# Low parts of y, of the output weights and of the late weights computed on VectorE instead of POOL, and the seventh pair's y split where it is gated

## The chip, the cores and the metric

The kernel runs on one core of a Trainium2 chip. Its time is the device time of one execution in microseconds (us), taken as the median of several runs; lower is better. In the profile TensorE appears as PE (its weight loads as PEld), VectorE as DVE, ScalarE as ACT, GpSimd as POOL, and SyncE, which here only starts DMAs, as SP. Each engine works through its own list of instructions in order, so an instruction that waits holds up everything behind it on that engine.

## The reference

Two residual layers over a sequence of 1024 positions and a width of 1024, all in float32: a gated linear recurrence (RG-LRU, width 1536), then a forgetting attention with 16 heads of 64, each followed by an output projection, and a final RMS norm. Cut to what matters here:

```python
# layer 0
h = rms_norm(x, norm_g[0]);  u = h @ lru_w_in
xb, gate = u[..., :1536], u[..., 1536:]
xc = causal_depthwise_conv(xb, conv_w, conv_b)
r, i = sigmoid(block_diag(xc, wa, ba)), sigmoid(block_diag(xc, wx, bx))
a = exp(-8 * r * softplus(-a_param))
hs = scan(a, sqrt(1 - a*a) * (i * xc))        # h_t = a_t h_{t-1} + b_t
x = x + (hs * silu(gate)) @ lru_w_out
# layer 1
h = rms_norm(x, norm_g[1]);  q, k, v, gate, f = split(h @ fox_w_in)
p = softmax(q k^T / 8 + cum_q - cum_k, causal) # 16 heads
x = x + ((p @ v) * silu(gate)) @ fox_w_out
out = rms_norm(x, final_g)
```

## The kernel before

**Split operands.** Every large product is made of three matmuls. An operand z in float32 is split into a high part, `to_hi` (a cast to the type `F32R`), and a low part, `to_lo` (L85/L86: `lo = z - hi`). `gemm_steps` (L101 to L114) then issues, for each block of 128 weights, high times high (L111), low weights times high (L112) and high weights times low (L113), all into one accumulator. So each weight block of 128 by 512 elements needs one cast on ACT (L75) and one subtraction, and each activation needs the same. The helper `weights` (L95) reads a block from DRAM into a tile `wf`, casts it on ACT into `wh` and by default subtracts on POOL into `wl`.

**Layer 0** runs over 12 blocks n of 128 channels (the loop at L364). For each n: the input product `ups`, the gates of the block before (`gates`, PSUM tile `gate`), the y of the block before that (`outputs`, L325), the convolution (`conv`: `us`, `xc`, the split `xch`/`xcl`), the gate-path product `gps`, `silu`, and the recurrence (`recur`, with a scan on DVE). `outputs` multiplies the scan's result by the gate and splits it into `yh` and `yl`, tiles of 128 by 1024. After each second block, `project_out(g)` becomes a list of pieces (`fill`) that are worked off between the blocks: for four pairs of output blocks, `out_weights` (L336) loads and splits 128 by 512 output weights, and four accumulations into `ops` are added to `x`. There are six groups g; groups 0 to 4 go through `project_out`, the last is done at L432. `held` is a dictionary of open `gps` tiles; at L411 it is set to `None`, and `out_weights` looks at that to choose the engine of its low part: VectorE once `held` is `None`, POOL before.

**Layer 1** runs over the 16 heads in pairs (a pair is one block of 128 channels). For each head: `maxima` (scores tile `S` on PE, the row maximum on DVE at L664, the exponential with its sum on ACT at L667, and the row of maxima `mrow` at L673), then `weigh` (transposed scores `ST`, the exponential `p` on ACT at L734 or L737, masking on POOL at L742, its split `ph`/`pl` on DVE at L81 and L86, and the product with V into `O`, L762 and L763). Then `scale` (L701) multiplies the gate path by the reciprocal sums on POOL, after those came through DRAM (`recd`, `recb`), and `gated` (L771) multiplies the head pair's output `yo` by that on POOL, at every odd head and for each half c of the sequence. For pairs 0 to 6 the result is stored in DRAM (`y1d`); `load_y` reads it back later into a tile of tag `xp` and `split_y` splits it into `yhh`/`yhl`, cast on ACT and subtraction on DVE. The last pair, heads 14 and 15, is split directly from `yo`. `run` weaves these generators by the strings in `ORDERS`: digits name a generator, each `.` takes a piece of filler (projections for later pairs; from head 13 on `partial`, the output projection over the first six pairs, with tiles `xp`, `wh`, `wl`) and one of a side list. At head 14 the side list is `late` (L892): it loads and splits the output weights of the last two pairs (`woh` on ACT, `wol` on POOL; 4 blocks of 128 by 512), and then loads and splits the seventh pair's y (pair 6) for both halves. `final` uses pairs 6 and 7.

**Order.** The code is written in one order, but a planner that runs at build time (the context is made with `schedule_with_timeline_sim=True`) fixes the order on each engine: it takes, in written order of precedence, what its own simulation finds ready. `tc.issue_after(x)` holds instructions back until behind x on x's engine. On the chip that order is kept whatever the real durations are.

Of the kernel before, what the change touches and what calls it, by code (L numbers as in the profile page):

```python
# [33 lines left out]
def f32(ap):  # L34
    return ap.bitcast(F32)
# [3 lines left out]
def trunk(ctx: ExitStack, tc: tile.TileContext, xt, w0, wg, wo0, pc, gn, w1, wv, wf, bf, wo1, out):  # L39
    nc = tc.nc  # L40
# [31 lines left out]
    def to_hi(hi, src, eng, scale=None):  # L72
        if eng is nc.scalar:
            if scale is None:
                nc.scalar.copy(hi, src)  # L75
            else:
                nc.scalar.activation(hi, src, AF.Copy, scale=scale)
        elif eng is nc.gpsimd:
            nc.gpsimd.tensor_scalar(hi, src, 1.0 if scale is None else scale, 0.0, ALU.mult, ALU.add)
        elif scale is None:  # L80
            eng.tensor_copy(hi, src)  # L81
        else:
            eng.tensor_scalar(hi, src, scale, None, ALU.mult)

    def to_lo(lo, src, hi, eng):  # L85
        return eng.tensor_tensor(lo, src, f32(hi), ALU.subtract)  # L86
# [30 lines left out]
    def drain(gen):  # L117
        for _ in gen:
            pass
# [49 lines left out]
    with ExitStack() as l0:  # L169
# [57 lines left out]
        def split_x(h, layer=0):  # L227
            for k, (hi, lo) in enumerate((raw, hT)[layer][h]):
                g_ = gnt[:, layer, k : k + 1]
                x = xs[h][k]  # L230
                to_hi(hi, x, nc.scalar, scale=g_)
                nc.vector.scalar_tensor_tensor(lo, x, g_, f32(hi), ALU.mult, ALU.subtract)
                yield
# [91 lines left out]
        def outputs(n, parts=(slice(0, SEQ),), gate=itertools.repeat(None)):  # L325
            s = state.pop(n)
            y = tuple(ypool.tile([P, SEQ], F32R, tag=z, name=z) for z in ("yh", "yl"))
            for cs, _ in zip(parts, gate):
                a_ = s["a"][:, cs]
                nc.vector.tensor_tensor(a_, a_, s["sg"][:, cs], ALU.mult)  # L330
                yh, yl = (z[:, cs] for z in y)
                to_hi(yh, a_, nc.scalar)
                to_lo(yl, a_, yh, nc.vector if len(parts) > 1 else nc.gpsimd)
            ys.append(y)

        def out_weights(g, d0):  # L336

            wt = wpool.tile([P, 4, P], F32, tag="wf", name="wf", bufs=3)
            for j in range(2):
                nc.sync.dma_start(wt[:, 2 * j : 2 * j + 2], wo0[d0 + j, :, 2 * g : 2 * g + 2])  # L340
            hi = wpool.tile([P, 4, P], F32R, tag="wh", name="wh")
            lo = wpool.tile([P, 4, P], F32R, tag="wl", name="wl")
            to_hi(hi, wt, nc.scalar)
            to_lo(lo, wt, hi, nc.vector if held is None else nc.gpsimd)
            return [[(hi[:, 2 * j + i], lo[:, 2 * j + i]) for i in range(2)] for j in range(2)]

        def project_out(g):

            for d0 in range(0, KT, 2):
                for db, w in enumerate(out_weights(g, d0), d0):  # L350
                    for h, cs in enumerate(halves):
                        pt = ps.tile([P, HALF], F32, tag="g", name="ops")
                        gemm(pt, zip(w, [tuple(z[:, cs] for z in p) for p in ys[2 * g : 2 * g + 2]]))
                        x = xs[h][db]
                        nc.vector.tensor_tensor(x, x, pt, ALU.add)  # L355
                        yield
# [6 lines left out]
        ys, fill, held = [], iter(()), {}  # L363
        for n in range(NB):  # L364
# [8 lines left out]
            if n == 0:  # L373
                gps = held[0] = two_banks("gps")
                product(gps[:, 0], 0, first[1])
                for _ in zip(split_x(1), square_x(1)):
                    pass
                done = rms_row(sums[0], rs[:, :HALF])[1]
            else:
                gates(n - 1)  # L380
                if n > 1:
                    with tc.issue_after(state[n - 1]["last"].ins):
                        outputs(n - 2)
# [24 lines left out]
        for h in range(2):  # L408
            product(gps[:, h], h, wn)
        outputs(NB - 2)  # L410
        held = None  # L411
        drain(fill)
        recur(NB - 1, halves)
        outputs(NB - 1, halves, silu(state[NB - 1], gps, halves))
# [11 lines left out]
        def mm3(o, w, x, start, stop):  # L426
# [3 lines left out]
            nc.tensor.matmul(o, wh, xl, start=False, stop=stop)  # L430

        wl = [w for d0 in range(0, KT, 2) for w in out_weights(NB // 2 - 1, d0)]  # L432
        for h, cs in enumerate(halves):
            y = [tuple(z[:, cs] for z in p) for p in ys[-2:]]
            hT[h] = [pair() for k in range(KT)]
            parts = split_x(h, 1)
# [29 lines left out]
    with ExitStack() as l1:  # L466
# [76 lines left out]
        def kq_units(pair, hs=(0, 1)):  # L543

            for is_k in (1, 0):
                if hs[0] == 0:
                    kq[pair, is_k] = tuple(
                        kqpool.tile([P, SEQ], F32R, tag=f"qk{p}{is_k}", name=f"qk{p}") for p in "hl"
                    )
                hi, lo = kq[pair, is_k]  # L550
                eng = nc.vector if pair == 0 else nc.scalar

                def use(h, pt):
                    cs = slice(h * HALF, (h + 1) * HALF)
                    if is_k:
                        to_hi(hi[:, cs], pt, eng)
                        to_lo(lo[:, cs], pt, hi[:, cs], nc.vector)
                    else:
                        to_hi(hi[:, cs], pt, eng, scale=0.125)
                        nc.vector.scalar_tensor_tensor(lo[:, cs], pt, 0.125, f32(hi[:, cs]), ALU.mult, ALU.subtract)  # L560

                yield from project(is_k * 8 + pair, use, hs)
# [30 lines left out]
        parts = [at.tile([HEADS, SEQ], F32R, tag=t, name="cp") for t in ("ph", "pl")]  # L593
# [177 lines left out]
        def gated(hd, c, sub=slice(0, HALF)):  # L771

            if hd % 2 == 0:
                return
            pair = hd // 2
            yo = yos[pair, c][:, sub]
            nc.gpsimd.tensor_tensor(
                yo, yo, sgs[pair][:, c * HALF + sub.start : c * HALF + sub.stop], ALU.mult
            )
            if hd == 15:  # L780
                split_y(c, yo, nc.vector, sub)
            else:
                nc.sync.dma_start(y1d[c, pair], yo)
# [19 lines left out]
        def split_y(c, y, eng, sub=slice(0, HALF)):  # L803
            if sub.start == 0:
                y1[c].append(tuple(hpool.tile([P, HALF], F32R, tag=t, name="y" + t) for t in ("hh", "hl")))
            yh, yl = (z[:, sub] for z in y1[c][-1])
            to_hi(yh, y, nc.scalar)
            to_lo(yl, y, yh, eng)

        def load_y(c, pairs):  # L810
            for pair in pairs:
                y = at.tile([P, HALF], F32, tag="xp", name="y", bufs=3)
                nc.sync.dma_start(y, y1d[c, pair])
                split_y(c, y, nc.vector)
# [77 lines left out]
        def late():  # L892

            for half in range(2):
                wh, wl = (kqpool.tile([P, 8, P], F32R, tag=f"qk{p}{half}", name=f"wo{p}") for p in "hl")
                for b in range(2):
                    wt = wpool.tile([P, 4, P], F32, tag="wf", name="wf", bufs=3)
                    for d in range(2):
                        nc.sync.dma_start(wt[:, 2 * d : 2 * d + 2], wo1[half * 4 + b * 2 + d, :, 6:8])
                    sl = slice(4 * b, 4 * b + 4)  # L900

                    with tc.issue_after(seen[0].ins):
                        to_hi(wh[:, sl], wt, nc.scalar)
                    to_lo(wl[:, sl], wt, wh[:, sl], nc.gpsimd)
                    yield
                late_w.extend([(wh[:, 2 * d + k], wl[:, 2 * d + k]) for k in range(2)] for d in range(4))
            for c in range(2):
                load_y(c, [6])
                yield

        drain(kq_units(0, (1,)))
        fill = g_units(0)
        for _ in range(4):
# [5 lines left out]
        for hd in range(HEADS):  # L919
# [14 lines left out]
            if hd == HEADS - 1:  # L934
                break
            scale(hd)
            gated(hd, 0)
            side = late() if hd == 14 else iter(())
            run(second, weigh(hd, 1), maxima(hd + 1, 0), fill=fill, side=side)
            drain(side)  # L940
            gated(hd, 1)
            if hd == 12:

# [8 lines left out]
        quarters = [slice(0, 256), slice(256, HALF)]  # L952
        scale(15, slice(0, HALF))
        gated(15, 0)
        run("0.....0...0.......0...", weigh(15, 1, quarters[0]), fill=fill)
        drain(fill)
# [82 lines left out]
```

## Time and profile before

| | us |
|---|---|
| median of three runs (lowest, highest) | 1171.12 (1170.85, 1172.95) |
| the profiled execution | 1169.07 |
| its span, first to last instruction | 1167.4 |
| busy in that span: PE, PEld, DVE, ACT, POOL | 1135.0, 949.2, 821.0, 596.3, 394.5 |

The span leaves 1.7 us of the profiled execution outside it, and the profiled execution is 2.05 us below the median. The granted clock of PE is 0.992 on average over the span. A busy share is an average: what a place in the kernel is worth is read from the idle time of PE around it, since PE works on the same matmuls in any case.

### The profile page before, as it was taken

To read this page: it belongs to the slowest core of one execution; us is meant where nothing else is said; L and a number is where in the kernel's file an instruction comes from. 1 tells how busy PE (TensorE), PEld (TensorE's weight loads), DVE (VectorE), ACT (ScalarE), POOL (GpSimd) and SP (SyncE) were. 2 spreads that over 40 slices of the span, in tenths; PEclk is the share of its full clock that TensorE was granted. 3 is DMA by queue.
4 is the path that set the end of the run, shared out by engine and by line. 5 is a ranking of instruction groups with operands and counts; after the bars stand their busy time and mean duration, and the time that the engine had idled before them with its cause. 6 is when DMAs were issued, how large, how long until landed. Compare 5 with 4: busy or idle time off the path is not lost.

```text
span 1167.4 us, 15836 instructions
## 1 busy us (share of the span) xinstructions
PE 1135.0 (97%) x5653; PEld 949.2 (81%) x5653; DVE 821.0 (70%) x1278; ACT 596.3 (51%) x1010; POOL 394.5 (34%) x361
## 2 busy tenths in 40 slices
PE   9998999999999999999999999999999999999996
PEld 7786888888888887978888988889888898787795
DVE  7588746766567779566877767777577775676677
ACT  8386445364453667454554545545455454444343
POOL 1233332342323302342333332333333233143445
PEclk9999999999999999999999999999999999999998
DMA  6111120111111124441343423433234331656544
GB/s 209 51 41 40 51 59 28 59 50 41 55 36 55 54 68 153 108 132 46 92 118 81 102 64 92 119 85 89 64 91 110 90 84 60 184 161 171 160 134 145
DMA packets 63278, 105.95 MB, mean 91 GB/s; under 512 B 8856, under 2 KB 27928, under 8 KB 63200
## 3 DMA queue, kind: packets, MB, share of 16 engines
q1 hardware_dynamic: 63200, 104.95, 32.1%
q8 instruction: 44, 0.72, 0.3%
q14 instruction: 34, 0.28, 0.1%
HBM read 63.30 MB, written 16.45 MB: 68 GB/s over the span
## 4 chain that ended last, share of the span: by engine, by line
PE 48%; DVE 6%; ACT 2%; issue 2%; DMA 1%; DVEq 0%; POOL 0%; ACTq 0%; SPq 0%
PE gps L111 6%; PE gps L112 6%; PE gps L113 6%; PE O L763 3%; PE S L660 3%; PE S L659 3%; PE ST L728 3%; PE O L762 3%; PE ST L729 2%; PE vps L524 2%; PE vps L522 2%; PE vps L523 2%; PE ops L112 2%; PE ops L113 2%; PE ops L111 2%
## 5 line engine op out<-in xcount | busy, mean ns | idle before, releaser
L86 POOL TENSOR_TENSOR wl<-wf,wh 128x512 fp32r<-128x512 f32 (+2 forms) x148 | 216.5, 1467 | 418.3 <-ACT wh L75 376.2
L111 PE MATMUL gps<-hh,wh 128*128 128x512 f32 x576 | 226.9, 394 | 0.6 <-DVE qkl L560 0.5
L112 PE MATMUL gps<-hh,wl 128*128 128x512 f32 x576 | 227.4, 395 | 0.0
L113 PE MATMUL gps<-hl,wh 128*128 128x512 f32 x576 | 227.2, 394 | 0.0
L75 ACT CAST wh<-wf 128x512 fp32r<-128x512 f32 (+2 forms) x156 | 94.1, 607 | 134.6 <-PE ops L113 38.8
L667 ACT ACTIVATE S<-S,st 128x128 f32<-128x128 f32 (+7 forms) x128 | 91.4, 714 | 111.5 <-DVE st L664 110.6
L113 PEld LDWEIGHTS gps<-hl,wh 128*128 128x128 f32 x576 | 108.4, 188 | 24.6 <-issue 0.5
L81 DVE CAST ph<-p 128x512 fp32r<-128x512 f32 (+2 forms) x130 | 83.9, 655 | 61.4 <-ACT p L734 32.3
L111 PEld LDWEIGHTS gps<-hh,wh 128*128 128x128 f32 x576 | 108.5, 188 | 22.6 <-DVE qkl L560 0.9
L112 PEld LDWEIGHTS gps<-hh,wl 128*128 128x128 f32 x576 | 108.4, 188 | 21.9 <-POOL wl L86 0.3
L86 DVE TENSOR_TENSOR pl<-p,ph 128x512 fp32r<-128x512 f32 (+2 forms) x130 | 115.1, 901 | 2.2
L742 POOL TENSOR_SCALAR_AFFINE_SELECT p<-p 128x128 f32<-128x128 f32 (+1 forms) x128 | 46.9, 384 | 190.4 <-ACT p L734 92.0
L664 DVE CUSTOM_DVE_ANT_0 S<-S,mask 128x128 f32<-128x128 f32 (+7 forms) x128 | 96.6, 758 | 9.9 <-PE S L660 8.9
L355 DVE TENSOR_TENSOR x<-x,ops 128x512 f32<-128x512 f32 x80 | 54.3, 682 | 48.7 <-PE ops L113 48.4
L111 PE MATMUL ups<-hh,wh 128*128 128x512 f32 x192 | 76.3, 397 | 2.6 <-DVE us L265 1.9
L112 PE MATMUL ups<-hh,wl 128*128 128x512 f32 x192 | 75.6, 394 | 0.8 <-POOL wl L86 0.8
L113 PE MATMUL ups<-hl,wh 128*128 128x512 f32 x192 | 76.0, 396 | 0.2
L734 ACT ACTIVATE p<-ST 128x512 f32<-128x512 f32 (+1 forms) x68 | 53.0, 786 | 42.5 <-PE ST L729 39.1
L524 PE MATMUL vps<-wl,hh 128*128 128x256 f32 (+1 forms) x256 | 72.2, 284 | 0.7 <-POOL wl L86 0.7
L522 PE MATMUL vps<-wh,hh 128*128 128x256 f32 (+1 forms) x256 | 72.5, 285 | 0.0
L523 PE MATMUL vps<-wh,hl 128*128 128x256 f32 (+1 forms) x256 | 72.5, 284 | 0.0
L728 PE MATMUL ST<-U,T 128*128 128x512 f32 (+1 forms) x198 | 67.7, 349 | 2.7 <-ACT S L667 2.7
(193 smaller groups left out, 2611.1 us busy)
## 6 DMA issues: line engine op xcount, KB each, us to landing
wf<-in_w SPq DMA_DIRECT2D x100, 256.0 KB
wf<-in_wo SPq DMA_DIRECT2D x64, 128.0 KB
T<-qkh SPq DMA_DIRECT2D x28, 256.0 KB
U<-qkh SPq DMA_DIRECT2D x28, 256.0 KB
x<-in_xt SPq DMA_DIRECT2D x16, 256.0 KB
x1d<-x SPq DMA_DIRECT2D x16, 256.0 KB
wf<-in_wv SPq DMA_DIRECT2D x16, 256.0 KB
xp<-x1d SPq DMA_DIRECT2D x16, 256.0 KB
```

The source lines that it names most:

```text
L75: nc.scalar.copy(hi, src)
L81: eng.tensor_copy(hi, src)
L86: return eng.tensor_tensor(lo, src, f32(hi), ALU.subtract)
L111: nc.tensor.matmul(o, wh, xh[:, cs], start=i == 0, stop=False)
L112: nc.tensor.matmul(o, wl, xh[:, cs], start=False, stop=False)
L113: nc.tensor.matmul(o, wh, xl[:, cs], start=False, stop=i == len(pairs) - 1)
L522: nc.tensor.matmul(pt, xh, wh, start=k == 0, stop=False)
L523: nc.tensor.matmul(pt, xl, wh, start=False, stop=False)
L524: nc.tensor.matmul(pt, xh, wl, start=False, stop=k == KT - 1)
L664: nc.vector.tensor_tensor_reduce(S[:, :n], S[:, :n], mask[:, SEQ - n :], -1.0, -NEG, ALU.add, ALU.min, accum_out=m)
L667: seen[0] = nc.scalar.activation(S[:, :n], S[:, :n], AF.Exp, bias=f32(m), scale=-1.0, accum_out=sums[:, i : i + 1])
L728: nc.tensor.matmul(A[:, jj, :n], T[s][:, 0, ks], U[s][:, 0, q0:end], start=True, stop=False)
```

## The change

Four edits. `outputs` computes `yl` on VectorE always (before: on POOL, except for the last block, which comes in two halves). `out_weights` computes its low part on VectorE always (before: on POOL until `held` is `None`), and the line `held = None` goes. `late` computes the low part of the late weights on VectorE instead of POOL. And `gated` splits y directly for heads 13 and 15 instead of 15 alone, so pair 6 is no longer stored to `y1d` and read back, and `late` no longer loads it.

```diff
@@ outputs
-                to_lo(yl, a_, yh, nc.vector if len(parts) > 1 else nc.gpsimd)
+                to_lo(yl, a_, yh, nc.vector)
@@ out_weights
-            to_lo(lo, wt, hi, nc.vector if held is None else nc.gpsimd)
+            to_lo(lo, wt, hi, nc.vector)
@@ after the loop of layer 0
         outputs(NB - 2)
-        held = None
         drain(fill)
@@ gated
-            if hd == 15:
+            if hd >= 13:
                 split_y(c, yo, nc.vector, sub)
             else:
                 nc.sync.dma_start(y1d[c, pair], yo)
@@ late
-                    to_lo(wl[:, sl], wt, wh[:, sl], nc.gpsimd)
+                    to_lo(wl[:, sl], wt, wh[:, sl], nc.vector)
                     yield
                 late_w.extend([(wh[:, 2 * d + k], wl[:, 2 * d + k]) for k in range(2)] for d in range(4))
-            for c in range(2):
-                load_y(c, [6])
-                yield
-
```

## The prediction

> **What bounds the kernel now.** I read the busy times first, then a table of stretches, then PE's own waits.
>
> ```profile
> PE 1135.0 (97%) x5653; PEld 949.2 (81%) x5653; DVE 821.0 (70%) x1278; ACT 596.3 (51%) x1010; POOL 394.5 (34%) x361
> ```
>
> ```profile
> 108.00:112.00 4.00, 3.66 (x9) 2.53 (x10) 3.65 (x2) 3.42 (x6) 2.70 (x2) 0.57 0.00 0
> 120.00:150.00 30.00, 30.00 (x132) 24.39 (x130) 20.07 (x22) 9.18 (x12) 11.41 (x6) 1.00 0.13 41
> 1036.00:1056.00 20.00, 20.00 (x97) 16.80 (x96) 13.91 (x21) 7.23 (x15) 10.71 (x12) 1.00 0.63 166
> 1074.00:1084.00 10.00, 7.02 (x30) 4.91 (x31) 9.97 (x7) 4.29 (x8) 9.35 (x7) 1.00 0.40 117
> 1084.00:1089.00 5.00, 5.00 (x18) 3.88 (x19) 4.94 (x12) 2.42 (x5) 2.81 (x4) 0.66 0.80 238
> ```
>
> A row of the second fence is a stretch, its length, then busy us (and instructions) of PE, PEld, DVE, ACT and POOL, PE's granted clock, the DMA share and GB/s. PE is busy 97% of the span, so at most 1167.4 - 1135.0 = 32 us of idle time and a few us of low clock can be won. From 120 us on, PE is full (30.00 of 30) while DVE has 10 us of 30 free: a faster low part there moves nothing. Two places stand out where instructions leave POOL: 96 to 112 us (layer 0, blocks 2 and 3) and 1068 to 1089 us (head 14, where `late` runs). After each the clock falls, to 0.57 over 4 us and 0.66 over 5 us: (1 - 0.57) x 4 = 1.7 us and (1 - 0.66) x 5 = 1.7 us. PE's waits in the two places, by what ended them:
>
> ```profile
> PE gate L111 <- ACT ti L290: 2.2, 1, 2.2
> PE gate L111 <- ACT th L290: 1.9, 1, 1.9
> ```
>
> ```profile
> PE ST L728 <- ACT S L667: 1.8, 1, 1.8
> PE mrow L673 <- DVE st L664: 1.7, 1, 1.7
> PE S L659 <- ACT S L667: 0.6, 1, 0.6
> PE O L762 <- DVE ph L81: 0.6, 1, 0.6
> ```
>
> A row gives us in total, times and the longest. So the early place costs 4.1 us of waiting plus 1.7 of clock, 5.8 together; the late one 4.7 plus 1.7, 6.4 together. These 12 us are what the change can reach.
>
> **The change, part by part.** First the price of the moved subtractions.
>
> ```profile
> L86 POOL TENSOR_TENSOR yl<-a,yh x11: 2392/2406/3121, 85.7 to 410.4; 128x1024 fp32r<-128x1024 f32 x11
> ```
>
> ```profile
> L86 DVE TENSOR_TENSOR wl<-wf,wh x8: 676/681/691, 4.6 to 441.0; 128x512 fp32r<-128x512 f32 x8
> ```
>
> ```profile
> 103.90 0.43 DVE L86 TENSOR_TENSOR wgl<-wgf,wgh 128x256 fp32r<-128x256 f32 x1
> 104.25 1.22 DVE L86 TENSOR_TENSOR xcl<-xc,xch 128x1024 fp32r<-128x1024 f32 x1
> 108.32 1.23 DVE L319 SCALAR_TENSOR_TENSOR ti<-ti,xc 128x1024 f32<-128x1024 f32 x1 [2.86 <-ACT ti L290]
> ```
>
> Eleven `yl` leave POOL (2.41 us each) for DVE, where the same shape (`xcl`) takes 1.22: 13.4 us. Of the 24 blocks of output weights, DVE already does six (its eight `wl` less two at the start of the kernel), so 18 move at 0.68: 12.2 us. Four late blocks: 2.7. DVE gains 28 us of work over 1167.
>
> *Layer 0 after 120 us.* The eleven `yl` lie some 32 us apart (85.7 to 410.4), so one block brings one of them and about two weight blocks, 1.22 + 1.36 = 2.6 us, against 10 us free; PE's full rows cover it, and I cost it at nothing. Without that cover a subtraction on the path would cost its own 0.68 or 1.22.
>
> *The early place.* POOL and DVE get in each other's way:
>
> ```profile
> 85.66 3.12 POOL L86 TENSOR_TENSOR yl<-a,yh 128x1024 fp32r<-128x1024 f32 x1 [5.23 <-ACT yh L75]
> 88.74 1.47 POOL L86 TENSOR_TENSOR wl<-wf,wh 128x512 fp32r<-128x512 f32 x1
> ```
>
> ```profile
> 86.44 2.62 DVE L86 TENSOR_TENSOR wgl<-wgf,wgh 128x256 fp32r<-128x256 f32 x1
> 88.99 2.30 DVE L319 SCALAR_TENSOR_TENSOR ti<-ti,xc 128x1024 f32<-128x1024 f32 x1
> ...
> 95.86 1.19 DVE L265 TENSOR_TENSOR us<-ups,rs 128x1024 f32<-128x1024 f32 x1
> ```
>
> ```profile
> 91.80 0.62 ACT L75 CAST wh<-wf 128x512 fp32r<-128x512 f32 x1 [3.33 <-DMA wf<-in_wo]
> ```
>
> `wgl` took 2.62 instead of 0.43 while POOL wrote `yl`, and `ti` 2.30 instead of 1.23 beside `wl`: 2.19 + 1.07 = 3.26 us lost on an unbroken row of DVE work that ends with `us` at 97.05. ACT's convolution step waits for `us`, and both gate waits of PE (1.9, 2.2) come behind it. With the change these 3.26 go, and one `yl` and two `wl` come (the second behind the cast quoted last), 1.22 + 2 x 0.68 = 2.58: `us` ends 0.68 earlier. Both ends: with both `wl` planned behind `us` the gain is 2.04; with DVE held at the second `wl`, until its cast ends at 92.42, some 1.2 us, `us` comes 0.5 later. I take 0.7 gained, the row nearest to the present order, and leave the second wait and the low clock as they are.
>
> *The late place, the detour of pair 6.* The chain of waits passes through the read of `y1d`:
>
> ```profile
> 1069.98 0.62 ACT L75 CAST yhh<-y 128x512 fp32r<-128x512 f32 x1 [3.02 <-DMA y<-y1d]
> 1070.62 0.56 ACT L667 ACTIVATE S<-S,st 128x384 f32<-128x384 f32 x1
> ```
>
> ACT idles 3.02 us for that read with the exponential L667 queued behind it, and PE's 1.8 us wait is for that exponential. With the split made where y is gated, neither read nor cast is there; the casts go to just behind the two gating products:
>
> ```profile
> 1037.52 2.40 POOL L704 TENSOR_TENSOR sg<-sg,recb 64x1024 f32<-64x1024 f32 x1 [2.54 <-DMA recb<-recd]
> ...
> 1041.56 1.29 POOL L777 TENSOR_TENSOR yo<-yo,sg 128x512 f32<-128x512 f32 x1
> ...
> 1052.84 1.30 POOL L777 TENSOR_TENSOR yo<-yo,sg 128x512 f32<-128x512 f32 x1
> ```
>
> From 1036 to 1056 the table of stretches has ACT busy 7.2 of 20 us, DVE 13.9 and PE full, so 0.62 on ACT and 0.69 on DVE for each half cost nothing; without that cover they would cost 2.6. Two stores, two reads and two tiles of tag `xp` go as well, out of SP's list and out of `partial`'s way. Gain 1.75 (1.8 in the row).
>
> *The late place, the late weights.*
>
> ```profile
> 1074.38 2.85 POOL L704 TENSOR_TENSOR sg<-sg,recb 64x1024 f32<-64x1024 f32 x1
> 1077.20 3.98 POOL L86 TENSOR_TENSOR wol<-wf,woh 128x512 fp32r<-128x512 f32 x2
> ```
>
> ```profile
> 1073.80 1.18 DVE L81 CAST ph<-p 128x1024 fp32r<-128x1024 f32 x1 [1.89 <-ACT p L734]
> 1075.02 3.30 DVE L86 TENSOR_TENSOR pl<-p,ph 128x1024 fp32r<-128x1024 f32 x1
> 1078.24 1.79 DVE L81 CAST ph<-p 128x1024 fp32r<-128x1024 f32 x1
> 1079.95 2.27 DVE L86 TENSOR_TENSOR yhl<-y,yhh 128x512 fp32r<-128x512 f32 x1
> 1082.15 0.69 DVE L664 CUSTOM_DVE_ANT_0 S<-S,mask 128x512 f32<-128x512 f32 x1
> ```
>
> ```profile
> 1034.99 0.70 DVE L81 CAST ph<-p 128x1024 fp32r<-128x1024 f32 x1 [1.98 <-ACT p L734]
> ```
>
> ```profile
> 1076.74 0.62 ACT L75 CAST woh<-wf 128x512 fp32r<-128x512 f32 x1 [1.42 <-DMA wf<-in_wo]
> ```
>
> The row at 1034.99 is `ph` undisturbed. Ahead of the row maximum at 1082.15 stand 1.18 + 3.30 + 1.79 + 2.27 = 8.54 us of DVE work. I leave `pl` at 3.30: it ends 1.1 us after POOL's gate scaling, which stays. Left are 0.70 + 3.30 + 0.70 = 4.70, plus none to four of the `wol` at 0.68 (some fit into the 1.89 us of idle time), up to 2.72. So the maximum comes 1.1 to 3.8 us earlier, against waits of 0.6 + 1.7 + 0.6 = 2.84 (sum of the unrounded waits). I take 2.0, with two blocks ahead. The longest wait left is then under 1 us, and the low clock behind it should not come: another 1.7. DVE's new wait is for ACT's `woh` cast, and behind it stand `ph`, `pl` and the maximum; ACT waited 1.42 us for a weight DMA ahead of one of them.
>
> By the Trainium skill ("SBUF — State Buffer", section "Who interferes with whom") DVE and POOL share one port pair under an exclusive lock held for a whole instruction; this agrees with `wgl` (0.43 to 2.62), and makes the stretch of `pl` the scaling's, as in the sum. If it belonged to the `wol` instead, `pl` would shrink to about the 1.22 of its shape and the gain on DVE's chain would be 2.1 larger.
>
> *Sum*: 0.7 + 1.75 + 2.0 + 1.7 = 6.15, so 1169.07 - 6.1 = 1163.0 for an execution like the profiled one. The median shown stands 2.05 above it: 1165.0.
>
> **The rivals.** *The low clock stays* (A2). The clock fell in the late place after waits of at most 1.7 us each, and not after the 1.8 at 1071 (clock 1.00 from 1074 to 1084); so a remaining short wait may still bring it. Then 1.7 is not won: 1166.7. The skill ("TensorE: Matmul & The Clock Gate", section "Part 1") has the clock fall after an idle window of about 3.4 us with free-running windows; here shorter waits sufficed, so the measurement decides.
>
> *The early place is cured too* (B). For it: both gate waits hang on one row of DVE work that has lost 3.26 us to POOL, and the planner would then see nearly true durations. Against: DVE gets 2.58 back. Without the waits and the low clock 5.8 is won there instead of 0.7: 1159.9.
>
> *Only the detour goes* (C). The `wol` and the wait for `woh` take the place of POOL's interference, and nothing is won early: 4.70 + 2.72 + 1.42 = 8.84 ahead of the maximum, as much as the 8.54 before. Then 1.75 is won: 1169.4.
>
> *Nothing moves* (E). The change does not do what it says if the planner puts the casts of pair 6 behind the same exponentials, or PE's next wait takes over the freed time: 1171.
>
> *Slower* (D): ACT is held by the cast of pair 6. It now stands in ACT's list and waits for POOL's gating, that for the scaling, and that for `recb` from DRAM (2.54 in the row at 1037.52). If the planner thinks the reciprocals come without that wait, it lists the cast too early, and exponentials of head 14 queue behind it. One hold is about that wait and the gating, 2.54 + 1.29 = 3.8, plus a low clock of 1.7: 5.5. With both halves held, 11.0 less the 6.1 won is 4.9: 1176. It decides the sign beyond 2.3 once the holds sum to 8.4. Against it: ACT's idle time around both.
>
> **How the numbers follow.** Forecast 0.38, A2 0.11, B 0.12, C 0.15, E 0.08, D 0.16. This kernel's measurement can tell some 0.2%, 2.3 us, from no change. Faster: forecast, A2 and B, 0.61. Same: C and E, 0.23. Slower: D, 0.16. The range runs from 1158 (B and two us) to 1174 (half of D); the likeliest case's own bounds are 1162 to 1168.
>
> **What would show it.** Right: no `y<-y1d` wait on ACT near 1070, no PE wait for L667 there, `ph` near 0.70 and `yhl` gone ahead of the maximum, clock 1.00 in 1084 to 1089, `us` about 0.7 earlier. Wrong: ACT waiting on POOL `yo` around 1042 or 1054, DVE waiting on `woh`, new gate waits of PE before 120, or a planner's order in which other stretches lose time.

## The result, and the profile after

| | us |
|---|---|
| before, median of six runs (lowest, highest) | 1171.22 (1170.67, 1172.95) |
| after, median of six runs (lowest, highest) | 1161.45 (1157.61, 1162.42) |
| after / before, 95% interval | 0.9905 [0.9893, 0.9918] |
| the profiled execution after, its span | 1157.61, 1155.8 |

The change saves 9.8 us of the median. The profiled execution is one of the two shortest of the six; the other four lie between 1161.35 and 1162.42. That gap is no part of the change: it is taken up in the last section.

The busy times of the page after, to be held against the same row of before:

```profile
PE 1129.7 (98%) x5653; PEld 946.9 (82%) x5653; DVE 828.2 (72%) x1311; ACT 596.3 (52%) x1010; POOL 336.3 (29%) x328
```

33 instructions and 58 us have left POOL, and 33 have come to DVE, whose busy time nevertheless rises by only 7 us. Their own work is 28 us by the prediction's prices, so about 21 us of stretched DVE instructions have gone.

The tables of stretches, of before for one stretch and of after. A row is a stretch, its length, then busy us (and instructions) of PE, PEld, DVE, ACT and POOL, PE's granted clock, the DMA share and GB/s. The late place begins some 6 us sooner after than before and ends some 12 us sooner, so 1066 to 1081 answers roughly to 1074 to 1089.

```profile
90.00:120.00 30.00, 25.10 (x100) 19.03 (x99) 26.39 (x20) 21.87 (x25) 9.46 (x5) 0.94 0.16 49
```

```profile
90.00:120.00 30.00, 30.00 (x130) 24.14 (x129) 25.82 (x26) 24.50 (x28) 6.64 (x4) 1.00 0.19 57
120.00:150.00 30.00, 30.00 (x131) 24.27 (x131) 21.70 (x23) 10.52 (x12) 6.12 (x4) 1.00 0.15 43
1030.00:1064.00 34.00, 32.89 (x156) 26.58 (x155) 24.24 (x45) 13.06 (x30) 11.24 (x14) 1.00 0.52 145
1066.00:1076.00 10.00, 9.29 (x44) 7.25 (x43) 9.97 (x10) 4.78 (x10) 7.08 (x6) 1.00 0.65 197
1076.00:1081.00 5.00, 4.69 (x23) 3.56 (x22) 4.83 (x11) 1.29 (x3) 1.67 (x4) 1.00 0.77 224
```

PE is now full in the early place, where it had 4.9 us idle and a clock of 0.94 over 30 us (1.8 us more). In the late place it is busy 9.29 of 10 us where it was 7.02, and the clock stays at 1.00. Only 1030 to 1064 is worse: 1.1 us of idle time, where the prediction's row of 1036 to 1056 had none.

PE's waits of after, the three largest groups; columns are us in total, times and the longest:

```profile
PE O L762 <- DVE pl L86: 3.3, 4, 1.0
PE rsrow L145 <- DVE rd L143: 3.2, 2, 1.7
PE ST L727 <- ACT S L666: 2.2, 3, 1.5
```

The two gate waits (2.2 and 1.9) are gone, and so are `mrow` (1.7) and the exponential's wait of 1.8 in the late place. What is left lies elsewhere: the longest `ST` wait at 1005 us, `rsrow` in the tail (before has the same row), and the `O` waits spread over the heads.

**Where the time came from.** PE does the same 5653 matmuls in every kernel of this study. Their order is nearly the same: the planner shifts single products by a few places (in the changed kernel, 541 of the 5653 places hold another product than before, all of them between 88 and 419 us or between 1063 and 1095). So I matched each trace's matmuls with those of before by the columns that they had moved, and read how much sooner PE reached the same point. The differences between two points say what a place gained (plus) or lost, in us. The places are in us of before's trace, and the last column ends at PE's last matmul. All figures come from one profiled execution each. The first instructions that the change moves are a `wl` at 73.22 us and a `yl` at 85.66.

| kernel | 0-90 | 90-120 | 120-1030 | 1030-1064 | 1064-1090 | behind 1090 | all |
|---|---|---|---|---|---|---|---|
| after | -0.1 | +7.1 | +1.0 | -2.0 | +6.5 | -0.4 | 12.0 |
| a1_yl | -2.5 | +6.8 | -0.3 | 0.0 | -1.6 | +0.1 | 2.5 |
| a2_wout | -1.7 | +0.5 | -1.0 | 0.0 | -0.3 | 0.0 | -2.5 |
| a3_pair6 | -0.4 | 0.0 | -0.7 | -1.3 | +1.1 | 0.0 | -1.4 |
| a4_late | -1.5 | -1.0 | +0.8 | 0.0 | +3.6 | -3.3 | -1.4 |
| g1_lateboth | -0.6 | 0.0 | -1.1 | -1.5 | +6.2 | -0.5 | 2.4 |
| b1_shadow | +0.1 | +1.2 | -1.4 | -1.4 | +6.1 | -3.9 | 0.8 |
| b2_scanfirst | -0.3 | +3.6 | +0.9 | -2.3 | +6.1 | -3.7 | 4.3 |
| f2_undo_wout | -0.4 | +6.1 | +0.2 | -1.6 | +6.3 | -4.0 | 6.7 |
| c1_again | -0.2 | +7.0 | +0.6 | 0.0 | +5.8 | -0.4 | 12.7 |
| e1_project | 0.0 | +7.0 | -3.3 | -1.4 | +6.1 | -5.0 | 3.5 |
| after_again | -0.6 | +7.0 | +0.6 | -1.9 | +6.5 | -3.8 | 7.8 |

The last row is the changed kernel on another chip, profiled in a longer execution: its places agree with the first row to 0.1, and to 0.4 from 120 to 1030, but for the ends, 0-90 and behind 1090. Differences in those two columns can't be put down to an edit.

**The early place.** DVE's timeline of after; columns are start, us, engine, line, operation, out<-in, and the idle time before with what ended it:

```profile
86.13 1.21 DVE L319 SCALAR_TENSOR_TENSOR ti<-ti,xc 128x1024 f32<-128x1024 f32 x1
87.26 0.41 DVE L86 TENSOR_TENSOR wgl<-wgf,wgh 128x256 fp32r<-128x256 f32 x1
87.60 1.21 DVE L86 TENSOR_TENSOR yl<-a,yh 128x1024 fp32r<-128x1024 f32 x1
88.73 1.21 DVE L321 TENSOR_TENSOR ti<-ti,m 128x1024 f32<-128x1024 f32 x1
89.87 1.21 DVE L265 TENSOR_TENSOR us<-ups,rs 128x1024 f32<-128x1024 f32 x1
91.00 2.27 DVE L322 TENSOR_TENSOR_SCAN a<-a,ti 128x1024 f32<-128x1024 f32 x1
93.20 0.66 DVE L86 TENSOR_TENSOR wl<-wf,wh 128x512 fp32r<-128x512 f32 x1
```

Before, the scan stood ahead of `us`, beside POOL's `wl` at 92.50, and PE had a third wait in this place, besides its two gate waits:

```profile
92.65 3.28 DVE L322 TENSOR_TENSOR_SCAN a<-a,ti 128x1024 f32<-128x1024 f32 x1
```

```profile
PE ups L112 <- POOL wl L86: 0.8, 1, 0.8
```

What POOL still does there after the change:

```profile
88.48 2.62 POOL L86 TENSOR_TENSOR wl<-wf,wh 128x512 fp32r<-128x512 f32 x1 [8.36 <-ACT wh L75]
```

There are four things to see. `wgl` and `ti` are at 0.41 and 1.21 (before: 2.62 and 2.30). `yl` costs 1.21, and the `wl` that came to DVE stands behind `us`. The scan, which stood ahead of `us` before and took 3.28, stands behind it now and takes 2.27. And a `wl` that stays on POOL starts at 88.48 beside `yl`: now it is the one that is stretched (1.29 undisturbed). `us` ends at 91.08 instead of 97.05: 5.97 us sooner, of which 0.31 is an earlier start of the row. PE's own changed order is not what frees the place: `a1_yl` below keeps PE's order of before up to 106 us, but for two matmuls, and gains 6.8 us; `a2_wout` has a changed order there and gains 0.5.

**The late place.** DVE's and POOL's timelines of after:

```profile
1063.62 1.90 DVE L86 TENSOR_TENSOR wol<-wf,woh 128x512 fp32r<-128x512 f32 x3 [0.21 <-ACT woh L75]
1065.58 0.69 DVE L81 CAST ph<-p 128x1024 fp32r<-128x1024 f32 x1
1066.31 1.22 DVE L86 TENSOR_TENSOR pl<-p,ph 128x1024 fp32r<-128x1024 f32 x1
1067.45 0.69 DVE L81 CAST ph<-p 128x1024 fp32r<-128x1024 f32 x1
1068.05 0.69 DVE L86 TENSOR_TENSOR wol<-wf,woh 128x512 fp32r<-128x512 f32 x1
1068.65 0.69 DVE L663 CUSTOM_DVE_ANT_0 S<-S,mask 128x512 f32<-128x512 f32 x1
```

```profile
1068.92 2.40 POOL L703 TENSOR_TENSOR sg<-sg,recb 64x1024 f32<-64x1024 f32 x1 [14.00 <-DMA recb<-recd]
```

From the first `ph` to the row maximum L663 DVE needs 0.69 + 1.22 + 0.69 + 0.69 = 3.29 us of work, against 8.54 before. This `pl` runs undisturbed, because POOL's scaling starts only behind the maximum's own start. The next `pl` stands beside the scaling and takes 3.21 us from 1069.26, but nothing on PE waits long for it.

**What was given back.** ACT's and DVE's timelines of after:

```profile
1035.47 0.62 ACT L75 CAST yhh<-yo 128x512 fp32r<-128x512 f32 x1 [5.40 <-POOL yo L776]
...
1048.99 0.62 ACT L75 CAST yhh<-yo 128x512 fp32r<-128x512 f32 x1 [2.09 <-POOL yo L776]
```

```profile
1036.13 0.69 DVE L86 TENSOR_TENSOR yhl<-yo,yhh 128x512 fp32r<-128x512 f32 x1 [2.53 <-ACT yhh L75]
1036.74 0.69 DVE L663 CUSTOM_DVE_ANT_0 S<-S,mask 128x512 f32<-128x512 f32 x1
...
1049.64 0.69 DVE L86 TENSOR_TENSOR yhl<-yo,yhh 128x512 fp32r<-128x512 f32 x1 [2.45 <-ACT yhh L75]
```

Both casts of pair 6 are listed ahead of the gating that they read, so ACT waits 5.40 and 2.09 us for POOL. DVE's `yhl` waits for the cast, and a row maximum of head 14 queues behind each `yhl` (at 1036.74 and 1050.36). This is the hold that the rival on the slower side described.

### The profile page after: what moved, and what is told of

It is laid out like the page before. It is cut to its first block, busy times and chain, and to the rows that moved or that the text cites. A ratio compares the mean times of both kernels' runs of the same rounds, so it can differ in the third digit from the quotient of the medians.

```text
span 1155.8 us, 15813 instructions
## 1 busy us (share of the span) xinstructions
PE 1129.7 (98%) x5653; PEld 946.9 (82%) x5653; DVE 828.2 (72%) x1311; ACT 596.3 (52%) x1010; POOL 336.3 (29%) x328
## 4 chain that ended last, share of the span: by engine, by line
PE 46%; DVE 6%; ACT 2%; DMA 2%; issue 1%; POOL 1%; DVEq 0%; ACTq 0%; SPq 0%; POOLq 0%
PE gps L111 6%; PE gps L113 6%; PE gps L112 6%; PE ST L727 3%; PE O L762 3%; PE S L659 2%; PE ST L728 2%; PE S L658 2%; PE O L761 2%; PE vps L523 2%; PE vps L521 2%; PE vps L522 2%; PE ops L111 2%; PE ops L113 2%; PE ops L112 2%
## 5 line engine op out<-in xcount | busy, mean ns | idle before, releaser
L86 POOL TENSOR_TENSOR wl<-wf,wh 128x512 fp32r<-128x512 f32 (+2 forms) x130 | 190.1, 1467 | 499.5 <-ACT wh L75 424.2
L666 ACT ACTIVATE S<-S,st 128x128 f32<-128x128 f32 (+7 forms) x128 | 91.4, 714 | 114.1 <-DVE st L663 113.1
L81 DVE CAST ph<-p 128x512 fp32r<-128x512 f32 (+2 forms) x130 | 80.0, 625 | 57.2 <-ACT p L733 30.1
L86 DVE TENSOR_TENSOR pl<-p,ph 128x512 fp32r<-128x512 f32 (+2 forms) x130 | 118.3, 927 | 2.4
L663 DVE CUSTOM_DVE_ANT_0 S<-S,mask 128x128 f32<-128x128 f32 (+7 forms) x128 | 96.6, 758 | 5.1 <-PE S L659 4.1
```

Of the source, the lines that this page charges most:

```text
L663: nc.vector.tensor_tensor_reduce(S[:, :n], S[:, :n], mask[:, SEQ - n :], -1.0, -NEG, ALU.add, ALU.min, accum_out=m)
L666: seen[0] = nc.scalar.activation(S[:, :n], S[:, :n], AF.Exp, bias=f32(m), scale=-1.0, accum_out=sums[:, i : i + 1])
```

## The experiments

All times are medians beside before on the same chip. The ratio and its interval are those on record for the runs, not the quotient of the two medians.

### One edit at a time: which edit frees which place

`a1_yl`, before with the first edit alone:

```diff
-                to_lo(yl, a_, yh, nc.vector if len(parts) > 1 else nc.gpsimd)
+                to_lo(yl, a_, yh, nc.vector)
```

> Only yl on VectorE. Theory O (the planner's new order, us ahead of the scan, cures the early place; with yl alone the planned order has that already): early place 6 to 7 us gained, no gate wait of PE over 0.5 us before 120, total near 1164. Theory L (POOL's interference alone): only the 2.19 us stretch of wgl goes, 1.07 of ti beside wl stays: 1 to 3 us gained, total 1168 to 1170. Late place unchanged under both.

1165.06 against 1170.78, ratio 0.9945 [0.9926, 0.9963]. The early place gains 6.8 of the 7.1 us. In its trace `us` stands ahead of the scan, as in the changed kernel. So moving the eleven `yl` alone frees the early place, while the output weights are where they were before.

`a2_wout`, before with the second edit alone:

```diff
-            to_lo(lo, wt, hi, nc.vector if held is None else nc.gpsimd)
+            to_lo(lo, wt, hi, nc.vector)
```

> Only the output weights' low parts on VectorE; in the planned order the scan of block 1 stays ahead of us, as before. Theory O: the two gate waits stay, 0 to 1 us gained, total 1170 to 1171. Theory L: POOL's wl no longer stretches ti, yl still stretches wgl: 1 to 3 us gained, total 1168 to 1170.

1171.67 against 1170.78, 0.9998 [0.9987, 1.0008]: nothing. PE's waits in the early place and DVE's timeline there:

```profile
PE gate L111 <- ACT ti L290: 2.3, 1, 2.3
PE gate L111 <- ACT th L290: 1.3, 1, 1.3
```

```profile
87.30 3.45 DVE L319 SCALAR_TENSOR_TENSOR ti<-ti,xc 128x1024 f32<-128x1024 f32 x1
90.67 1.51 DVE L86 TENSOR_TENSOR wgl<-wgf,wgh 128x256 fp32r<-128x256 f32 x1
```

POOL's `yl`, 2.41 us from 87.25 on, is still there and stretches `ti` by 2.2; the `wl` behind it on POOL, 1.76 us from 90.14 on, stretches `wgl` by 1.1. That `wl` is a block of the input products, which no edit moves.

`a3_pair6`, before with the fourth edit alone:

```diff
-            if hd == 15:
+            if hd >= 13:
...
-            for c in range(2):
-                load_y(c, [6])
-                yield
```

> Only pair 6 split where it is gated. My step: the 1.75 us wait for L667 behind the y1d read goes and the rest of the late place stays: total 1169 to 1170, or 1167.5 where the low clock goes with it. Rival: the casts that wait for POOL's gating give 2 to 2.6 us back between heads 13 and 14, so the total is 1171 to 1172.

1170.93 against 1170.78, 1.0005 [0.9993, 1.0018]: nothing, which is less than the 1.75 that I had priced. The wait of 1.8 for the exponential is gone (0.4 at 1061 us stands behind the second of the casts that now wait for the gating), but another has come in the late place:

```profile
PE O L763 <- DVE pl L86: 3.6, 1, 3.6
```

```profile
1078.55 5.75 DVE L86 TENSOR_TENSOR pl<-p,ph 128x1024 fp32r<-128x1024 f32 x1
```

```profile
1077.54 2.73 POOL L704 TENSOR_TENSOR sg<-sg,recb 64x1024 f32<-64x1024 f32 x1 [1.21 <-DMA recb<-recd]
...
1080.73 1.25 POOL L86 TENSOR_TENSOR wol<-wf,woh 128x512 fp32r<-128x512 f32 x1
1081.95 2.92 POOL L86 TENSOR_TENSOR wl<-wf,wh 128x512 fp32r<-128x512 f32 x2
```

One `pl` of 5.75 us lies beside an unbroken row on POOL, with a `wol` in it. That the detour's gain needs the `wol` to leave POOL as well is borne out by `g1_lateboth`, below.

`a4_late`, before with the third edit alone:

```diff
-                    to_lo(wl[:, sl], wt, wh[:, sl], nc.gpsimd)
+                    to_lo(wl[:, sl], wt, wh[:, sl], nc.vector)
```

> Only the late weights' low parts on VectorE. My step: with the y1d read still there, the row maximum comes 1 to 2 us earlier, the 1.75 wait stays: 1 to 3.7 us gained (with the low clock), total 1167.5 to 1170. Rival: wol stands on VectorE ahead of the masked exponentials' split and pair 6's yhl is still there, so nothing is gained: 1171 to 1172.

1168.25 against 1170.78, 0.9972 [0.9961, 0.9984]. The late place gains 3.6. PE still waits 1.4 us for the exponential behind the read of `y1d`, and 1.7 for a `ph` that takes 2.70 us.

`g1_lateboth`, both of these edits and neither of the early ones:

```diff
-            if hd == 15:
+            if hd >= 13:
...
-                    to_lo(wl[:, sl], wt, wh[:, sl], nc.gpsimd)
+                    to_lo(wl[:, sl], wt, wh[:, sl], nc.vector)
...
-            for c in range(2):
-                load_y(c, [6])
-                yield
```

> Both edits of the late place and neither of the early ones: pair 6 split where it is gated and the late weights' low parts on VectorE. Theory (alone, the detour's removal gave +1.1 us between 1064 and 1090 and the late weights' move +3.6, because each left a wait of the other kind; together all of it goes): +6 to +6.5 there, -2 between 1030 and 1064 for the casts that wait for POOL's gating, nothing from 90 to 120 us, so 1166 to 1168. Rival (the two only add up, and the rest of the late gain comes from the early edits' change of order): +4.7 there, so 1168 to 1169.5.

1167.86 against 1171.02, 0.9975 [0.9964, 0.9986]. The late place gains 6.2, more than 1.1 + 3.6: each edit alone leaves the other's wait to take over. But 1.5 of it is given back ahead of it, so both edits together are worth 3.2 us of the median, hardly more than `a4_late` alone (2.5).

### The early place: interference, order, or both

`b1_shadow` is the changed kernel with a subtraction on POOL in each block, of about the shape that left, into a tile that nothing reads. PE and DVE keep the changed kernel's order up to about 110 us.

```diff
...
-                to_lo(yl, a_, yh, nc.vector)
+                to_lo(yl, a_, yh, nc.vector); len(parts) == 1 and nc.gpsimd.tensor_tensor(shadow, rs[:, :960], f32(yh)[:, :960], ALU.subtract)
```

> The changed kernel plus, for each of the first eleven blocks, a POOL subtraction of 128 by 960 beside yl (rs minus the high part of y, into a tile that nobody reads). PE's and VectorE's planned order is the same up to 110 us. Theory L: wgl and its neighbours are stretched by 2 us again and gate waits of PE come back before 110: 1161.5 plus 3 to 6. Theory O: VectorE is stretched but us stays ahead of the scan, PE waits under 1 us before 110: 1161.5 to 1163.

1167.56 against 1171.16, 0.9971 [0.996, 0.9982]. The early place keeps 1.2 of its 7.1 us. POOL's and DVE's timelines, then PE's waits there:

```profile
85.39 2.75 POOL L333 TENSOR_TENSOR shadow<-rs,yh 128x960 f32<-128x960 f32 x1 [5.45 <-ACT yh L75]
```

```profile
85.94 3.28 DVE L319 SCALAR_TENSOR_TENSOR ti<-ti,xc 128x1024 f32<-128x1024 f32 x1
89.15 1.52 DVE L86 TENSOR_TENSOR wgl<-wgf,wgh 128x256 fp32r<-128x256 f32 x1
```

```profile
PE ops L113 <- DVE yl L86: 2.3, 1, 2.3
PE ups L111 <- ACT wh L75: 1.0, 1, 1.0
PE gate L111 <- ACT th L290: 0.5, 1, 0.5
```

DVE does the same work as in the changed kernel, and nothing waits for `shadow`. Its mere presence on POOL adds 2.07 us to the first `ti`; `wgl` then comes so late that the `wl` on POOL starts ahead of it (88.27 to 90.39) and adds 1.11. `us` ends 3.0 us later than in the changed kernel, and waits of 3.8 us in all and a mean clock of 0.94 over 90 to 120 us are back. That `shadow` holds up POOL's own work is not the cause: the next `wl` behind the second `shadow` starts 0.57 us after it, when ACT's cast is ready. That the interference matters is thereby shown, not argued.

`b2_scanfirst` is the changed kernel with one thing put back: `us` of block 3 behind the scan of block 1.

```diff
+                with (tc.issue_after(scans[1].ins) if n == 3 else ExitStack()): nc.vector.tensor_tensor(us[:, cs], pt, rs[:, cs], ALU.mult)
...
```

> The changed kernel with us of block 3 held behind the scan of block 1 on VectorE, the order of before, and no yl or wout on POOL. Theory O: the scan's 2.3 us come back ahead of us, and gate waits of 2 to 4 us with them: 1164 to 1166. Theory L: without POOL's stretch us ends 3 us before its old time anyway, PE waits under 1 us: 1161.5 to 1162.5.

1162.04 against 1171.16, 0.9931 [0.9914, 0.9947]. In the trace the early place gains 3.6 instead of 7.1. DVE's timeline and PE's wait:

```profile
90.23 3.27 DVE L322 TENSOR_TENSOR_SCAN a<-a,ti 128x1024 f32<-128x1024 f32 x1
93.42 1.19 DVE L265 TENSOR_TENSOR us<-ups,rs 128x1024 f32<-128x1024 f32 x1
```

```profile
PE gate L111 <- ACT ti L290: 1.6, 1, 1.6
```

`us` ends at 94.61, between 91.08 and 97.05, one gate wait remains, and a low clock behind it. So the scan's new place is worth about half of the early gain in this profile. The two causes do not add up: the interference alone takes back 5.9 of the 7.1 us (`b1_shadow`) and the order alone 3.5, since each makes `us` late enough for waits. And part of what the order brings back is interference again: the scan stands beside POOL's `wl` (2.68 us from 88.67) and takes 3.27 instead of 2.27. The ratios to before, 0.9931 here and 0.9905 for the change, say about 3 us as well, with intervals that overlap.

`f2_undo_wout` is the changed kernel with the second edit undone, the other three kept:

```diff
-            to_lo(lo, wt, hi, nc.vector)
+            to_lo(lo, wt, hi, nc.vector if held is None else nc.gpsimd)
...
+        held = None
```

> The changed kernel with the low parts of the output weights back on POOL, all else kept. Theory (the detour of y's subtraction alone frees the early place; the output weights' part is worth 0 to 1 us, as when it was done alone): 1161 to 1162.5, and no wait over 1 us of TensorE for the gate's operands between 96 and 112 us. Rival (POOL's two output weight subtractions, beside VectorE's tensor instructions there, stretch them enough to bring a wait and a low clock back): 1163 to 1165, with a group of ti or yl at 2 us or more beside POOL's wgl.

1162.46, against 1159.37 of the changed kernel (`after_again`) and 1169.96 of before on the same chip; 0.9929 [0.9915, 0.9942]. The early place loses 0.9 of 7.0. PE's wait and POOL's timeline there:

```profile
PE ups L112 <- POOL wl L86: 0.9, 1, 0.9
```

```profile
105.76 5.14 POOL L86 TENSOR_TENSOR wl<-wf,wh 128x512 fp32r<-128x512 f32 x2 [10.54 <-ACT wh L75]
```

The wait ends with the first of these two `wl`, at 107.61. It is a block of the input products, which this edit leaves where it was: it takes 1.85 us here and 1.88 in the changed kernel. Here its cast on ACT comes 1.3 us later (105.08 against 103.77), and PE gets there only 0.4 us later. The theory holds by place and in that no gate wait comes back, and the rival's stretched `ti` is not there; but the 0.9 us have a cause that neither named. They are not safely the price of the edit either: `a1_yl`, with the same order on PE up to 1058 us and the output weights on POOL too, gains 6.8 and waits 0.3 us for the same block. Beside DVE's `yl`, `ti` and scan it is POOL that loses: its two `wl` from 89.08 on take 2.89 and 3.30 us instead of 1.29. The next product on DVE, at 94.17, then pays in turn (2.13 instead of 1.21).

By the medians the second edit is worth 3.1 us on top of the other three, with intervals that overlap and no place in the profile that accounts for it; alone it is worth nothing (`a2_wout`).

### The hold of the casts

`c1_latesplit` and `c1_again` (the same kernel, on two chips) are the changed kernel with pair 6's two splits put behind the last exponential L666 of a later run, so that ACT reaches them when POOL's gating is done:

```diff
-            if hd >= 13:
+            if hd == 15:
...
+            if hd == 14:
+                with tc.issue_after(seen[0].ins):
+                    split_y(1, yos[6, 1], nc.vector)
...
+            if hd == 13:
+                with tc.issue_after(seen[0].ins):
+                    split_y(0, yos[6, 0], nc.vector)
```

> The changed kernel with pair 6's casts put behind an exponential of head 14 (half 0 after the next head's first maxima, half 1 after head 14's second ones) instead of right behind the gating. If the casts' waits for POOL's gating give back the 1.9 us seen at 1041 and 1052, those go: 1159.5 to 1160.5. Rival: the loss there has another cause (the masking and scaling on POOL), nothing changes: 1161 to 1162.

1160.21 against 1171.16, 0.9904 [0.9882, 0.9927]: by its time no better than the change. By place it does what was meant, 0.0 between 1030 and 1064, and its profiled execution lost 2.0 us ahead of 90 us and 4.0 behind 1090. So it ran again beside the changed kernel.

> The changed kernel itself, once more on this chip, as the measure for the other two runs: 1161 to 1162 us as the median, single runs from 1157.5 to 1162.5. By the comparison of the traces it gains about 7 us between 96 and 120 us, about 6.5 between 1064 and 1090, and gives back about 2 between 1030 and 1064.

> The changed kernel with the two casts of pair 6's y put behind exponentials of head 14, timed beside the changed kernel. Theory (the 2.0 us given back between 1030 and 1064 are ScalarE held by casts that wait for POOL's gating): 1.5 to 2 us below the changed kernel of the same chip, so 1159.5 to 1160.5. Rival (the hold only moves idle time that TensorE makes up by 1090): the same time as the changed kernel within 0.5 us.

The changed kernel took 1159.37 us (1158.57 to 1160.54), this one 1156.49 (1155.71 to 1160.49); against before 0.9901 [0.9886, 0.9917] and 0.9886 [0.9869, 0.9903]. ACT's timeline of `c1_again`, and its stretch:

```profile
1034.93 0.66 ACT L666 ACTIVATE S<-S,st 128x512 f32<-128x512 f32 x1 [4.21 <-DVE st L663]
...
1036.05 0.62 ACT L75 CAST yhh<-yo 128x512 fp32r<-128x512 f32 x1 [0.34 <-POOL yo L776]
```

```profile
1030.00:1064.00 34.00, 34.00 (x165) 28.35 (x164) 25.11 (x48) 14.98 (x32) 11.18 (x14) 1.00 0.54 145
```

The exponential comes 2.65 us sooner than in the changed kernel (1034.93 against 1037.58), the casts wait 0.34 and not at all, and PE is full. The mechanism is shown: 1.9 us were given back there, and late casts avoid it. That the whole kernel is faster than the change is likely (2.9 us between the medians of one chip) but not settled, since the intervals overlap, and since the tail behind 1090, which the edit is not meant for, differs by 3.4 us between the two profiled executions.

### Moving more: the other weights

`e1_project`, the changed kernel with the projection weights of layer 1 on DVE too:

```diff
-            w = list(weights(w1[cb_i]))
+            w = list(weights(w1[cb_i], lo_eng=nc.vector))
```

> The changed kernel with the low parts of layer 1's projection weights on VectorE as well (48 more subtractions of 0.68 us). If POOL's wl stretches pl at the starts of heads (waits of 0.7 to 1.0 at 578, 723, 868), these go and 2 to 3 us are gained: 1158.5 to 1159.5. Rival: VectorE, at 23 of 30 us in layer 1, becomes the bound: 1162 to 1168.

1164.38 against 1171.16, 0.9951 [0.9932, 0.9971]: slower than the change. PE's waits from 520 to 1000 us, first of the changed kernel, then of this one:

```profile
PE O L762 <- DVE pl L86: 2.5, 3, 1.0
```

```profile
PE O L762 <- DVE pl L86: 3.8, 3, 1.3
PE ST L727 <- ACT S L666: 2.7, 4, 1.8
```

Between 120 and 1030 us it loses 4.3 against the change. The theory failed at its own places: near 578, 723 and 868 us the waits of 0.8, 1.0 and 0.7 grew to 1.3 each. At the first of them `pl` still takes 2.19 us, because with `wl` gone POOL's product `yo` has moved up beside it (1.62 us from 578.61). And a new wait of 1.8 us comes at 557: ahead of the row maximum on DVE there now stand a `wl` (0.68) and `qkl` (0.69), which the planner had put behind the maximum in the changed kernel. Moving to DVE pays where it frees a chain on DVE from POOL; here it lengthened the chain, and POOL's next instruction took the place of the one that left.

## Why the prediction was right, and where its steps failed

The forecast was 1165.0 with a range of 1158 to 1174; the median came to 1161.45. Sign and range held, but 1161.45 is outside the likeliest case's own bounds of 1162 to 1168, and the terms of the sum were not right one by one: 6.15 us were forecast, 9.8 came. In the profile the early place alone gave 6.4 us more than its term and the late place 1.1 more, while 2.0 were given back that the sum had at nothing. That these did not leave the range was in part luck.

- **The early place, 0.7: mis-sized, and the largest error.** It gave 7.1. The stretches of `wgl` and `ti`, 3.26 together, are gone (by the starts of the rows 3.5), but my reason holds for the first alone. The `wl` at 88.74, which stretched `ti`, is a block of the input products (loaded from `in_w` at 80.46) and not of the output weights. The change leaves it on POOL, where it now starts behind DVE's `yl` and is stretched itself. So of the two `wl` that I priced on DVE only one moves, and the planner put it behind `us`. And I kept the order of the scan: its 3.2 us left the row ahead of `us` too, 1.0 of them again a stretch, by the output weights' `wl` at 92.50. The row's sum is -3.5 (interference) + 1.1 (`yl`) - 3.2 (scan), which with a gap of 0.1 gives the 5.7 us by which it is shorter. I took "the row nearest to the present order", and "leave the second wait and the low clock as they are" followed from that. With `us` 6 us sooner both gate waits and the low clock go. This is rival B's mechanism. Its price of 5.8 was also short: PE's idle time and clock in that stretch were worth 6.7, because a third wait goes, 0.8 us for a `wl` that stood behind the second `yl` in POOL's list (109.30 to 111.79).
- **Layer 0 behind 120 us, nothing: right.** PE is full from 120 to 150, DVE has 8 us of 30 free, and 120 to 1030 moved by 1.0.
- **The detour, 1.75, and the casts at nothing: right in the wait, wrong in the cover.** The 1.8 us wait is gone. But I read the cover from busy shares (ACT busy 7.2 of 20 us), while what counts is where the cast stands in ACT's list: it waited 5.40 and 2.09 us for POOL. That is rival D's mechanism, and it was in the prediction with 3.8 us and a low clock for each hold. PE lost 1.9 to both holds together: the clock stayed at 1.00, and part of ACT's wait was idle time anyhow. `c1_again` shows both the cause and the remedy.
- **The late weights, 2.0: right in sign, too small.** The figure did not follow from its own rows: with two blocks ahead they leave 8.54 - 4.70 - 1.36 = 2.48. And I left `pl` at 3.30 because POOL's scaling stays. It stays, but later: before, the copy of the reciprocals stood 4.3 us ahead of ACT's three `woh` casts (1066.94 and 1071.19), and now stands 0.2 behind them (1063.13 and 1062.97). The copy starts the detour that the scaling waits for, and behind the casts on ACT stands the exponential that `pl` waits for. So the `pl` ahead of the maximum took 1.22.
- **The low clock of the late place, 1.7: right.** The stretch is at 1.00; rival A2 did not occur. The three late terms give 5.45 against 6.5 measured, less the 1.9 given back ahead.
- **The prediction as a sum of edits** also hides that they are not independent: by the medians the detour is worth nothing alone, the late weights 2.5 us, both together 3.2; the output weights nothing alone, and beside the other three edits 0.9 in the early place and 3.1 by the medians, neither of them settled.

The Trainium skill ("SBUF — State Buffer", section "Who interferes with whom"), which has the two engines exclude each other, agrees with `b1_shadow` (`wgl` 0.41 to 1.52, `ti` 1.21 to 3.28) and with `f2_undo_wout`, where POOL pays (1.29 to 2.89).

## What to carry to other kernels

A subtraction that is off the path on POOL is not free: price it by the rows on DVE that it lies beside, and look at whether a chain that PE waits for runs through them, and at which of the two instructions starts first. When an edit changes the durations that a planner sees, price the order ahead of the critical instruction anew, at both ends, instead of keeping it. And a cover is a place in an engine's list, not a busy share: ask what the moved instruction will be waiting for when its turn comes.

## What the hardware showed that I had not expected

- Which of the two engines pays is told by which instruction starts first. I took DVE's subtractions and products of 128 by 1024 (`ti`, `yl`, `xcl`, `pl`; 1.22 us when alone) in all fourteen traces, and the subtractions and products on POOL that overlap them. Of the 216 that began while POOL's was running, 207 were stretched, and all but one of these ended 1.1 to 1.2 us after POOL's had ended, as if they had begun only then. Of the 154 that began ahead of POOL's none took over 1.23 us, and the `wl` on POOL beside them took up to 2.89 instead of 1.29. Eight of the nine others began while POOL's instruction was itself still behind an earlier one of DVE (as `ti` at 88.73 in the changed kernel, behind `yl`), and the ninth overlapped by under 0.1 us. The one that ended later is the `pl` of 5.75 us in `a3_pair6`: when POOL's scaling was over, four more instructions of POOL's row went ahead of it. Why they did there and nowhere else, no run here shows.
- The clock fell behind one gate wait of 1.6 us (`b2_scanfirst`: 0.69 over 108 to 112 us), but in the same kernel it may fall or not. The changed kernel's two profiled executions, a stretch in the tail behind a wait for `rsrow` that both have (1.7 and 1.9 us in its longest):

```profile
1140.00:1144.00 4.00, 4.00 (x34) 3.61 (x32) 3.86 (x9) 1.75 (x6) 2.31 (x3) 1.00 0.37 127
```

```profile
1140.00:1144.00 4.00, 4.00 (x23) 4.00 (x24) 3.56 (x8) 1.74 (x5) 3.18 (x4) 0.59 0.19 66
```

  In the second the tail runs at a low clock from here on, in the first only from 1144 on (0.55 over 1144 to 1148), and the second loses 3.4 us. That is about the gap between the short and the long runs of the change; what decides it stays open.
